# Experts' down product in plain float32 with four column groups, and the steps around it, in a two-block network on one core

## Chip, cores and metric

One core of a Trainium2 chip runs the whole program. The metric is the device time of one execution in microseconds. A profiled execution gives a trace besides; its times are from its first to its last instruction.

## The reference

Two blocks of two layers each work on 256 tokens of 1024 features in float32. Only the last layer's last step matters here, a mixture of eight experts with 1536 hidden features of which each token takes two:

```python
def swiglu(h, w_gate, w_up, w_down):
    return (jax.nn.silu(h @ w_gate) * (h @ w_up)) @ w_down

def moe_swiglu(h, router, w_gate, w_up, w_down):
    probs = jax.nn.softmax((ht @ router).astype(F32), axis=-1)
    top_p, top_i = lax.top_k(probs, TOP_K)
    top_p = top_p / jnp.sum(top_p, axis=-1, keepdims=True)
    gates = jnp.sum(jax.nn.one_hot(top_i, N_EXPERTS, dtype=F32) * top_p[..., None], axis=1).astype(h.dtype)
    for e in range(N_EXPERTS):
        out = out + gates[:, e:e + 1] * swiglu(ht, w_gate[e], w_up[e], w_down[e])
```

## The kernel before

All products but one kind are computed in three float32r matmuls (`mm3`, lines 312 to 316): both operands are split into a high part (a copy by ACT) and a low part (a subtraction by DVE), and high x high, high x low and low x high are summed in PSUM. `wload` (lines 298 to 310) loads a weight unit into a `raw` buffer (three of 8 KB per partition) and splits it into `wh` and `wl` buffers (five each of 4 KB). The exception is the experts' up product, which is in plain float32 already.

The experts' layer is `moe` (from line 1379). For each expert at most CAP = 96 tokens are gathered with a one-hot matrix `oh`; if an expert has more, the program runs `experts` again with a base of 96 and of 192, each behind a branch (`tc.If`, line 1652). With these inputs neither branch is taken. The loop at line 1614 orders the work of expert `e`:

- `up(e)`, line 1518: the gathered tokens `xg` (features on partitions, 96 tokens as three tiles of 32) are the stationary operand, and the weights stream. Four column groups of 32 of the array work on four column ranges of 384 weights at once. Sixteen `mw` tiles (8 k steps of gate and up weights, 768 KB each, 512 KB for expert 0) are loaded by SP into seven buffers. Its six PSUM banks ("up" banks) are then all full; SiLU on ACT and a product on DVE empty them into three `u` tiles.
- Beside `up(e)` stand `scatter(e - 2)` (line 1596), which brings an expert's rows back to the tokens with two matmuls each for the high and low part, and updates `x` with the gate on DVE, and for every odd `e` the gather of the next pair of experts (line 1500), both in a second set of two banks ("dn"). They are called at odd k steps.
- `down(e - 1)`, line 1570: 12 blocks of 128 hidden features; per block two halves of 512 output columns, each an `mm3` with the turned hidden features (`ph`, `pl`, 128 x 96) as the stationary operand, so 72 matmuls. At its end `oh` is turned (`ohT`), and the two accumulators are split into `yh` and `yl`.
- `turn(e)`, line 1542: nine transposes bring the `u` tiles to features on partitions, through three "up" banks, and a split makes `ph` and `pl`. The following `up(e + 1)` uses the same banks.

After the loop come `down(7)`, in it `scatter(6)`, and then `scatter(7)`, which also writes the output. The order of PE's instructions is that of the code (`manual_schedule` with `MAN`); the order on ACT, DVE and on SP, which issues the loads, is a planner's. Every engine takes its own instructions in order. `places` makes the one-hot tiles, and `first_up` computes the first third of expert 0's hidden features for all tokens before the loop.

Of the kernel before, what the change touches and what calls it, by code (L numbers as in the profile page):

```python
# [37 lines left out]
MW_BUFS = 7  # L38
# [140 lines left out]
def pack(i):  # L179
# [32 lines left out]
    a["mo_d"] = units_cols(i["moe_down_2"][0].reshape(NE * DE, D), 2, D)  # L212
# [10 lines left out]
def build(tc, a, out, stages=None):  # L223
# [7 lines left out]
    with ExitStack() as es:  # L231
# [1147 lines left out]
        def moe(more, head, next_head):  # L1379
            hT = nrm["h"]  # L1380
            with tc.tile_pool(name="moe", bufs=1) as sp:
# [74 lines left out]
                def first_up(mid):  # L1456
# [15 lines left out]
                    for t in range(2):  # L1472
                        u = sp.tile([P, 512], F32, tag="u", name="u", bufs=4)
# [13 lines left out]
                def experts(base, mid):  # L1487
# [10 lines left out]
                    xg, made, turned, back = {}, {}, {}, {}  # L1498

                    def gather(e, kind="dn"):  # L1500

                        xg[e // 2] = xgs[e // 2 % 2]
                        for k0 in range(0, KT, 2):
                            p = bank(kind)
# [8 lines left out]
                            for k in (k0, k0 + 1):  # L1513
                                src = grp(p[:, (k - k0) * S : (k - k0 + 1) * S], 2)[:, :, :CAP]
                                A.activation(xg[e // 2][:, k], src, AF.Copy, scale=nrm["g"][:, k : k + 1])
                            yield

                    def up(e):
# [4 lines left out]
                        h = xg[e // 2]  # L1523
                        o = [[bank("up") for _ in range(2)] for _ in range(NT)]
                        for k in range(KT):
                            for m in range(2):
                                w = sp.tile([P, DE], F32, tag="mw", name="mw", bufs=MW_BUFS)
                                nc.sync.dma_start(w[:, : 4 * n], a["mo_u"][(e * KT + k) * 2 + m][:, lo:])
                                for t in range(NT):
                                    l = h[:, k, e % 2, t * C32 : (t + 1) * C32]  # L1530
                                    for g in range(4):
                                        T.matmul(o[t][m][g * C32 : (g + 1) * C32, :n], l, w[:, g * n : (g + 1) * n],  # L1532
                                                 start=k == 0, stop=k == KT - 1, skip_group_check=True)
                            yield
                        made[e] = []
                        for t in range(NT):
                            u = sp.tile([P, 384], F32, tag="u", name="u", bufs=4)
# [4 lines left out]
                    def turn(e):  # L1542

                        ph = sp.tile([P, DE // P, CAP], F32R, tag="ph", name="ph", bufs=2)
                        pl = sp.tile([P, DE // P, CAP], F32R, tag="pl", name="pl", bufs=2)
                        turned[e] = (ph, pl)
                        k1 = 0
                        if e in mid:
                            k1 = 4
                            u = mid[e]  # L1550
                            for k0 in (0, 2):
# [9 lines left out]
                                split(ph[:, k0 : k0 + 2], pl[:, k0 : k0 + 2], grp(p, 2)[:, :, :CAP])  # L1561
                        c = (DE // P - k1) // 4
                        for t, u in enumerate(made.pop(e)):
# [3 lines left out]
                            part = lambda z: z[:, k1:, t * C32 : (t + 1) * C32].rearrange("p (g c) n -> p c g n", c=c)  # L1567
# [122 lines left out]
```

## Time and profile before

| | us |
|---|---|
| median of three runs (1708.68 to 1712.89) | 1708.85 |
| the profiled execution's own time | 1710.19 |
| its span, first to last instruction | 1708.3 |
| PE busy | 1636.6 (96%) |
| DVE busy | 1014.3 (59%) |
| ACT busy | 830.2 (49%) |
| DMA bytes | 335.11 MB, 196 GB/s over the span |

The rows below are of these views. The page's slices cut the span into 40 parts; a digit is the busy share in tenths. A row of the windows gives a stretch in us, its length, then for PE, PEld (weight loads), DVE, ACT and POOL the busy time with the number of instructions in brackets (engines without any are left out where a row is of one line alone), then PE's granted clock as a share of full speed, the busy share of the 16 DMA engines, and GB/s. A row of a timeline gives start, duration, engine, line and operation, what it writes from what, shapes and count, and in square brackets how long the engine stood idle before it and who ended that. A row of the chain gives start, duration and the step that the end hung on. A row of the waits gives who waited for whom, the total in us, how often, and the longest. Matmuls overlap in the records: the distance of their starts is what one costs, not the duration that is shown. A float32 product leaves two matmul records.

### The profile page before, as it was taken

What the parts mean: (1) busy time and instruction counts of PE and PEld (TensorE: products, weight loads), DVE (VectorE), ACT (ScalarE), POOL (GpSimd) and SP (SyncE); (2) the same over time, 40 slices, a digit from 0 to 9 for tenths busy, and PEclk for the clock granted to TensorE, in tenths of its full rate; (3) what the DMA queues carried; (4) which work ended last, traced back from release to release, by engine and by line L of the source; (5) the groups of instructions that cost most, each with busy time, mean ns of one, the idle gap of its engine ahead of it and who ended that gap; (6) DMA issues with size and microseconds to landing.
All of it is one profiled execution on the core that took longest, in us unless ns stands there. A gap on an engine that the chain in (4) does not pass through costs nothing.

```text
span 1708.3 us, 28919 instructions
## 1 busy us (share of the span) xinstructions
PE 1636.6 (96%) x11932; PEld 1323.4 (77%) x11932; DVE 1014.3 (59%) x1653; ACT 830.2 (49%) x1428; POOL 135.8 (8%) x158
## 2 busy tenths in 40 slices
PE   7999999999999999989999999989899999999995
PEld 5878999888889998989899998979764455445554
DVE  6767777676487776876565555875641344234434
ACT  6646555555475565653464445653532234124323
POOL 2100000021000001260000001440100000000000
PEclk9999999999999999989999999999999999999998
DMA  7433655455245544530265544410479998989963
GB/s 278 148 122 134 214 177 194 148 206 173 99 151 198 190 175 151 171 110 1 77 231 187 189 169 156 168 67 24 181 276 366 334 347 336 355 315 327 359 234 111
DMA packets 52580, 335.11 MB, mean 196 GB/s; under 512 B 6000, under 2 KB 6032, under 8 KB 25680
## 3 DMA queue, kind: packets, MB, share of 16 engines
q1 hardware_dynamic: 51120, 327.70, 53.2%
q0 software_dynamic: 736, 4.32, 0.7%
q8 instruction: 97, 1.59, 0.4%
q10 hardware_dynamic: 576, 1.08, 0.2%
q14 instruction: 51, 0.42, 0.1%
HBM read 332.03 MB, written 1.05 MB: 195 GB/s over the span
## 4 chain that ended last, share of the span: by engine, by line
PE 81%; DVE 5%; issue 5%; ACT 3%; DMA 3%; POOL 2%; DVEq 0%; ACTq 0%; POOLq 0%
PE pj L316 13%; PE pj L315 13%; PE pj L314 13%; PE pj L1532 9%; PE sm L314 5%; PE sm L316 5%; PE sm L315 5%; PE sm L1532 5%; DVE wl L307 2%; DMA raw<-in_mo_d 2%; PE sm L425 2%; PE sm L1151 2%; PE sm L1160 2%; ACT wh L306 1%; PE sm L1154 1%
## 5 line engine op out<-in xcount | busy, mean ns | idle before, releaser
L307 DVE TENSOR_TENSOR wl<-raw,wh 128x1024 fp32r<-128x1024 f32 (+2 forms) x448 | 538.1, 1212 | 228.5 <-ACT wh L306 224.4
L306 ACT CAST wh<-raw 128x1024 fp32r<-128x1024 f32 (+2 forms) x448 | 458.9, 1033 | 277.2 <-PE pj L315 102.2
L314 PE MATMUL pj<-hTh,wh 128*128 128x256 f32 x1192 | 336.1, 282 | 0.0
L315 PE MATMUL pj<-hTl,wh 128*128 128x256 f32 x1192 | 335.8, 282 | 0.0
L316 PE MATMUL pj<-hTh,wl 128*128 128x256 f32 x1192 | 335.3, 282 | 0.0
L314 PEld LDWEIGHTS pj<-hTh,wh 128*128 128x128 f32 x1192 | 227.1, 191 | 1.1
L315 PEld LDWEIGHTS pj<-hTl,wh 128*128 128x128 f32 x1192 | 227.2, 191 | 0.9
L316 PEld LDWEIGHTS pj<-hTh,wl 128*128 128x128 f32 x1192 | 226.8, 191 | 0.2
L1532 PE MATMUL pj<-mw,xg 128*32 128x384 f32 (+1 forms) x2048 | 183.7, 475 | 8.1 <-DVE pl L321 4.8
L314 PE MATMUL sm<-wh,ph 128*128 128x512 f32 (+1 forms) x456 | 179.7, 394 | 3.2 <-ACT ph L320 3.2
L315 PE MATMUL sm<-wl,ph 128*128 128x512 f32 (+1 forms) x456 | 179.3, 393 | 0.0
L316 PE MATMUL sm<-wh,pl 128*128 128x512 f32 (+1 forms) x456 | 177.8, 393 | 1.2 <-DVE pl L321 1.2
L1532 PEld LDWEIGHTS pj<-mw,xg 128*32 128x32 f32 x2048 | 64.3, 110 | 100.9 <-issue 81.3
L316 PE MATMUL pj<-wh,hTl 128*128 128x512 f32 (+1 forms) x368 | 137.9, 377 | 3.3 <-DVE hTl L328 3.3
L314 PE MATMUL pj<-wh,hTh 128*128 128x512 f32 (+1 forms) x368 | 139.2, 381 | 0.5 <-ACT hTh L326 0.4
L315 PE MATMUL pj<-wl,hTh 128*128 128x512 f32 (+1 forms) x368 | 137.5, 376 | 0.2 <-DVE wl L307 0.2
L1532 PE MATMUL sm<-mw,xg 128*32 128x384 f32 (+1 forms) x1024 | 102.3, 478 | 3.0 <-DVE pl L321 3.0
L314 PEld LDWEIGHTS sm<-wh,ph 128*128 128x128 f32 (+1 forms) x456 | 80.8, 177 | 30.4 <-issue 3.4
L316 PEld LDWEIGHTS sm<-wh,pl 128*128 128x128 f32 (+1 forms) x456 | 80.8, 177 | 25.5 <-DVE pl L321 1.6
L315 PEld LDWEIGHTS sm<-wl,ph 128*128 128x128 f32 (+1 forms) x456 | 80.7, 177 | 22.6
L836 DVE SCALAR_TENSOR_TENSOR u<-pj,tab_f,u 128x254 f32<-128x254 f32 (+1 forms) x176 | 82.8, 479 | 20.0 <-ACT u L834 18.2
L316 PEld LDWEIGHTS pj<-wh,hTl 128*128 128x128 f32 x368 | 69.5, 189 | 15.6 <-DVE hTl L328 6.1
(418 smaller groups left out, 2198.7 us busy)
## 6 DMA issues: line engine op xcount, KB each, us to landing
mw<-in_mo_u SPq DMA_DIRECT2D x112, 768.0 KB, 6.7
raw<-in_mo_d SPq DMA_DIRECT2D x48, 1024.0 KB, 5.3
raw<-in_up SPq DMA_DIRECT2D x44, 1024.0 KB, 4.8
raw<-in_dn SPq DMA_DIRECT2D x22, 1024.0 KB, 4.8
raw<-in_fg_u SPq DMA_DIRECT2D x22, 1024.0 KB, 4.8
raw<-in_od_b SPq DMA_DIRECT2D x18, 1024.0 KB, 4.8
raw<-in_hy_b SPq DMA_DIRECT2D x16, 768.0 KB, 4.3
raw<-in_hy_a SPq DMA_DIRECT2D x12, 1024.0 KB, 4.9
```

What stands on the lines that cost most here:

```text
L306: A.copy(h, r)
L307: V.tensor_sub(m, r, h.bitcast(F32))
L314: T.matmul(o, lh, rh, start=first, stop=False)
L315: T.matmul(o, lh, rl, start=False, stop=False)
L316: T.matmul(o, ll, rh, start=False, stop=last)
L425: T.matmul(q, hT[j][:, k, ts_], w[f][k][v], start=t + k + i == 0, stop=k == KT - 1 and i == 2, skip_group_check=True)
L836: V.scalar_tensor_tensor(u[:, g, sh:], q[:, : S - sh], cw[:, f, g, wi : wi + 1], u[:, g, sh:], op0=OP.mult, op1=OP.add)
L1151: T.matmul(pq[:, i * P : (i + 1) * P], Am[:, i], U[:, i], start=i == 0, stop=True, skip_group_check=True)
L1154: T.transpose(pt[:, i * P : (i + 1) * P], U[:, i], ident)
L1160: T.matmul(pu[:, i * P : (i + 1) * P], Tt[:, i], Q[:, i], start=i == 0, stop=True, skip_group_check=True)
L1532: T.matmul(o[t][m][g * C32 : (g + 1) * C32, :n], l, w[:, g * n : (g + 1) * n], start=k == 0, stop=k == KT - 1, skip_group_check=True)
```

## The change

`mo_d` is packed as plain rows of 128 x 1024 per block. The down product is float32 in four column groups: for each of the 12 blocks, four products of 512 columns (two tiles of 32 tokens x two halves of the output) into one bank, and four of 256 columns (the third tile of 32 tokens) into the other. Down weights are not split any more; they are loaded as 1 MB pairs into `raw` and as single 512 KB blocks into the `wh` and `wl` buffers. `turn` makes one float32 tile `uT` with ACT copies, and also turns the one-hot. The gather of the next pair and `turn(e)` are called inside `down(e - 1)`, in the "up" banks; half of the gather's evictions are on DVE. The accumulators are gathered into one tile `y` before the split into `yh` and `yl`. There are 8 `mw` buffers instead of 7, 3 `u` buffers instead of 4, and one `xg` tile instead of two. In the last expert the order of the last blocks is no longer a special one. The second overflow branch stands inside the first.

```diff
-MW_BUFS = 7
+MW_BUFS = 8
+Q = D // 4
...
-    a["mo_d"] = units_cols(i["moe_down_2"][0].reshape(NE * DE, D), 2, D)
+    a["mo_d"] = np.ascontiguousarray(i["moe_down_2"][0]).reshape(-1, P, D)
...
-                    def gather(e, kind="dn"):
-
-                        xg[e // 2] = xgs[e // 2 % 2]
+                    def gather(e):
+
                         for k0 in range(0, KT, 2):
-                            p = bank(kind)
+                            p = bank("up")
...
-                                A.activation(xg[e // 2][:, k], src, AF.Copy, scale=nrm["g"][:, k : k + 1])
+                                A.activation(o, src, AF.Copy, scale=g) if k0 % 4 else V.tensor_scalar_mul(o, src, g)
...
+                    def product(o, l, w, first, last):
+                        T.matmul(o, l, w, start=first, stop=last, skip_group_check=True)
...
-                                split(ph[:, k0 : k0 + 2], pl[:, k0 : k0 + 2], grp(p, 2)[:, :, :CAP])
+                                A.copy(uT[:, k0 : k0 + 2], grp(p, 2)[:, :, :CAP])
...
-                            split(part(ph), part(pl), p[:, : c * P].rearrange("p (c g n) -> p c g n", c=c, g=4))
...
+                            A.copy(uT[:, k1:, t * C32 : (t + 1) * C32].rearrange("p (g c) n -> p c g n", c=c),
+                                   p[:, : c * P].rearrange("p (c g n) -> p c g n", c=c, g=4))
...
-                            if w[kk] is None:
-                                w[kk : kk + 2] = wload(a["mo_d"][e * nk // 2 + kk // 2], 2, D)
-                            c = slice(n * 512, (n + 1) * 512)
-                            mm3(acc[n][:CAP], ph[:, kk], pl[:, kk], w[kk][0][:, c], w[kk][1][:, c], kk == 0, kk == nk - 1)
...
+                        for kk in range(nk):
+                            if kk % 4 == 0:
+                                raw = wbuf("raw", 2 * D, F32, RAW_BUFS)
+                                nc.sync.dma_start(grp(raw, 2), a["mo_d"][e * nk + kk : e * nk + kk + 2].rearrange("k p c -> p k c"))
+                                w += [raw[:, :D], raw[:, D:]]
+                            elif kk % 4 >= 2:
+                                one = wbuf(("wh", "wl")[kk % 2], D, F32, W_BUFS)
+                                nc.sync.dma_start(one, a["mo_d"][e * nk + kk])
+                                w.append(one)
+                            for g in range(4):
+                                t, c = g % 2, g // 2 * H
+                                product(acc[0][g * C32 : (g + 1) * C32], uT[:, kk, t * C32 : (t + 1) * C32],
+                                        w[kk][:, c : c + H], kk == 0, kk == nk - 1)
+                            for g in range(4):
+                                product(acc[1][g * C32 : (g + 1) * C32, :Q], uT[:, kk, 2 * C32 :], w[kk][:, g * Q : (g + 1) * Q],
+                                        kk == 0, kk == nk - 1)
+                            if kk % 2:
+                                yield
...
+                        y = sp.tile([P, D], F32, tag="y", name="y", bufs=1)
+                        A.copy(y[: 2 * C32, :H], acc[0][: 2 * C32])
+                        V.tensor_copy(y[: 2 * C32, H:], acc[0][2 * C32 :])
+                        for g in range(4):
+                            o, p = y[2 * C32 : CAP, g * Q : (g + 1) * Q], acc[1][g * C32 : (g + 1) * C32, :Q]
+                            V.tensor_copy(o, p) if g % 2 else A.copy(o, p)
+                        split(yh[:CAP], yl[:CAP], y[:CAP])
...
                         for k, _ in enumerate(up(e)):
                             if k % 2 == 1:
                                 next(side, 0)
                                 next(side, 0)
-                        rest(side)
+                        more_ = gather(e + 1) if e % 2 == 1 and e + 1 < NE else iter(())
                         if e:
-                            rest(down(e - 1))
-                        turn(e)
+                            for k, _ in enumerate(down(e - 1)):
+                                next(more_, 0)
+                                if k == 3:
+                                    turn(e)
+                        else:
+                            turn(e)
...
-                for base in (CAP, 2 * CAP):
-                    with tc.If(full > base):
+                with tc.If(full > CAP):
+                    with tc.manual_schedule(engines=MAN):
+                        experts(CAP, {})
+                    with tc.If(full > 2 * CAP):
                         with tc.manual_schedule(engines=MAN):
-                            experts(base, {})
+                            experts(2 * CAP, {})
```

## Rows read from the trace of the kernel before

**Rows 1.** The page's 40 slices: PE and DMA, busy tenths.

```profile
PE   7999999999999999989999999989899999999995
...
DMA  7433655455245544530265544410479998989963
```

**Rows 2.** Windows over the experts' loop: ups 0 and 1; the six middle experts.

```profile
1258.00:1316.40 58.40, 58.40 (x815) 30.54 (x807) 4.01 (x10) 8.36 (x21) 0.00 (x0) 1.00 0.97 369
1316.40:1649.80 333.40, 322.30 (x2918) 164.28 (x2914) 128.37 (x145) 102.32 (x142) 0.00 (x0) 0.99 0.89 331
```

**Rows 3.** Windows of 8 us: first 512 KB loads, then 768 KB loads.

```profile
1268.00:1276.00 8.00, 8.00 (x154) 4.81 (x148) 0.00 (x0) 0.00 (x0) 0.00 (x0) 1.00 1.01 387
1276.00:1284.00 8.00, 8.00 (x102) 4.95 (x98) 2.98 (x8) 2.62 (x8) 0.00 (x0) 1.00 1.01 417
```

**Rows 4.** Windows of line 1532 alone: an unhindered quarter, then six first quarters.

```profile
1346.53:1354.41 7.88, 7.88 (x96) 3.01 (x96) 1.00 0.96 364
1334.34:1345.40 11.06, 8.29 (x96) 2.81 (x96) 1.00 0.98 351
1389.13:1399.68 10.55, 8.29 (x96) 2.81 (x96) 1.00 0.95 344
1447.91:1456.85 8.94, 8.08 (x96) 2.93 (x96) 1.00 0.95 335
1500.58:1513.33 12.75, 9.96 (x96) 3.06 (x96) 0.87 0.86 295
1561.54:1570.55 9.01, 8.09 (x96) 2.91 (x96) 1.00 0.96 333
1614.29:1624.09 9.80, 8.29 (x96) 2.81 (x96) 1.00 0.98 367
```

**Rows 5.** PE's timeline at the start of up(3).

```profile
1390.75 0.85 PE L1532 MATMUL pj<-mw,xg 128*32 128x384 f32 x8 [0.76 <-ACT ohT L1589]
1393.09 2.14 PE L1532 MATMUL pj<-mw,xg 128*32 128x384 f32 x24 [1.49 <-DVE pl L321]
```

**Rows 6.** The chain that ended last, just ahead of these.

```profile
1387.47 1.06 ACT wh L306
...
1388.55 2.36 DVE wl L307 x2
```

**Rows 7.** The DMA queue's own waits, 1200 to 1708 us.

```profile
SPq L301 <- DVE wl L307: 177.2, 50, 17.1
```

**Rows 8.** A down product's window, line 314 alone (one of three).

```profile
1371.15:1387.84 16.69, 9.49 (x24) 3.86 (x24) 1.00 0.91 343
```

**Rows 9.** Windows of line 1532: 256 columns (up 0), 384 columns (half of up 2).

```profile
1257.23:1278.08 20.85, 20.85 (x384) 12.37 (x384) 1.00 0.98 373
1355.54:1371.15 15.61, 15.61 (x192) 6.13 (x192) 1.00 0.96 361
```

**Rows 10.** PE's timeline at the start of down(7).

```profile
1671.06 0.47 PE L314 MATMUL sm<-wh,ph 128*96 128x512 f32 x1 [3.17 <-ACT ph L320]
...
1672.93 0.74 PE L316 MATMUL sm<-wh,pl 128*96 128x512 f32 x1 [1.17 <-DVE pl L321]
1673.46 0.63 PE L314 MATMUL sm<-wh,ph 128*96 128x512 f32 x1
```

**Rows 11.** Window of one scatter insertion, line 1603 alone (half of it).

```profile
1399.68:1400.81 1.13, 0.89 (x2) 0.37 (x2) 1.00 0.60 178
```

**Rows 12.** Timelines of DVE and PE before up(0).

```profile
1251.93 3.51 DVE L307 TENSOR_TENSOR wl<-raw,wh 128x1024 fp32r<-128x1024 f32 x3
...
1256.09 0.38 PE L1509 MATMUL pj<-oh,xh 128*128 128x256 f32 x1 [1.30 <-DVE u L1475]
```

**Rows 13.** Timelines of ACT and DVE at the end.

```profile
1692.51 0.58 ACT L320 CAST yh<-sm 96x512 fp32r<-96x512 f32 x1 [2.19 <-PE sm L316]
...
1694.19 2.73 DVE L1605 SCALAR_TENSOR_TENSOR x<-pj,gates,x 128x512 f32<-128x512 f32 x4 [0.38 <-PE pj L1604]
```

**Rows 14.** SP's own waits at the branches.

```profile
SPq L1652 <- SPq L1652: 6.9, 2, 3.9
```

More of the change, by code (lines that the diff above doesn't have):

```diff
@@ L1542, in turn @@
                     def turn(e):
[L1544 to L1546 removed]
+                        uT = sp.tile([P, DE // P, CAP], F32, tag="uT", name="uT", bufs=2)
+                        turned[e] = uT
                         k1 = 0
@@ L1589, in down @@
                         A.copy(ohT[:CAP], p[:CAP, :S].rearrange("p (t n) -> p t n", t=2))
-                        yh = sp.tile([P, 2, 512], F32R, tag="yh", name="yh", bufs=1)
-                        yl = sp.tile([P, 2, 512], F32R, tag="yl", name="yl", bufs=1)
-                        for n in range(2):
-                            split(yh[:CAP, n], yl[:CAP, n], acc[n][:CAP])
-                        back[e] = (ohT, yh, yl)
+                        back[e] = ohT
+                    def down(e):
+                        uT = turned.pop(e)
+                        acc = [bank("dn"), bank("dn")]
+                        nk = DE // P
+                        H = 2 * Q
+                        w = []
+                        for kk in range(nk):
[16 more added lines that the diff above has]
+                                yield
+                        yh = sp.tile([P, D], F32R, tag="yh", name="yh", bufs=1)
+                        yl = sp.tile([P, D], F32R, tag="yl", name="yl", bufs=1)
+                        y = sp.tile([P, D], F32, tag="y", name="y", bufs=1)
[5 more added lines that the diff above has]
+                        split(yh[:CAP], yl[:CAP], y[:CAP])
+                        back[e] = (back[e], yh, yl)
@@ L1609, in scatter @@
                                 yield
-                    rest(gather(0, "up"))
+                    rest(gather(0))
                     for e in range(2, NE):
@@ L1614, in experts @@
                     for e in range(NE):
-                        side = iter(())
-                        if e >= 2:
-                            side = scatter(e - 2)
-                        if e % 2 == 1 and e + 1 < NE:
-                            side = chain(side, gather(e + 1))
+                        side = scatter(e - 2) if e >= 2 else iter(())
                         for k, _ in enumerate(up(e)):
@@ L1646, in moe @@
                 banks["dn"] = ([ps() for _ in range(2)], 0)
-                xgs = [xp.tile([P, KT, 2, CAP], F32, tag=tag, name="xg", bufs=2) for tag in ("xTh", "xTl")]
+                xg = xp.tile([P, KT, 2, CAP], F32, tag="xTh", name="xg", bufs=2)
                 with tc.manual_schedule(engines=MAN):
```

33 lines of the change are left out of this document (10 added, 23 removed).

## The prediction

> **What bounds the kernel now.** I read the page's slices first. PE is busy nearly everywhere, and only in the last quarter do DMA's digits also stand at 8 and 9 [rows 1]. That quarter is the experts' loop (1257 to 1692 us), the only part that the change touches, so the question is which of PE and DMA ends last there. The windows by stretch answer it: over the six middle experts (1316.4 to 1649.8) PE is busy 322.3 of 333.4 us, while DMA moves 331 GB/s at a share of 0.89 [rows 2]. The same DMA moved 417 GB/s between 1276 and 1284, where free buffers let the queue run full [rows 3]. So PE is the bound and DMA has room. Per expert the queue moves 16 x 0.786 + 12 x 0.524 = 18.9 MB: 45 us at 417 GB/s, where an expert takes 333.4 / 6 = 55.6 us.
>
> Why, then, is PE idle some 11 us there? The windows of the up product show it. A quarter of an up product (96 records; every plain float32 product leaves two) takes 7.88 us when nothing holds it, but the first quarter of ups 2 to 7 takes 8.94 to 12.75 [rows 4]. PE's timeline names the holder: the records wait for ACT's ohT copy (0.76 us) and DVE's pl split (1.49 us) [rows 5], that is, for the PSUM banks that `turn` has just filled. The chain of work says why these come late: in front of pl stand the copies and subtractions (wh 1.06, wl 2 x 1.18 us) of the down weights for the next expert, which ACT and DVE take in order [rows 6]. SP's loads wait for the same wl splits, 177.2 us in all [rows 7], which costs nothing while PE is the bound.
>
> **The change part by part.** (1) Down product. Now 72 matmuls in 16.69 us, 0.232 us each, of which one of three lines has 24 [rows 8]. After: per block kk four products of 512 columns and four of 256, each two records. The price of a record in four column groups: 20.85 / 384 = 54.3 ns for 256 columns, 15.61 / 192 = 81.3 ns for 384 [rows 9]. The step of 27.0 ns per 128 columns puts 512 at 108.3 ns. A block is 8 x 108.3 + 8 x 54.3 = 1301 ns, an expert 12 x 1.301 = 15.61 us: 1.08 us less, for eight experts **-8.6**. No row has 512 columns in four groups; the bounds are 81.3 ns (as at 384) and 0.232 us (today's 512-column record). I take 108.3, since the two rows lie on a line through almost zero.
>
> (2) The splits of the down weights go: per expert 12 on ACT and 12 on DVE. Neither engine is the bound, so their time itself brings nothing; what they delay does. The turn becomes plain ACT copies and stands after the eighth of twelve blocks of `down(e-1)`, so its evictions have four blocks (5.2 us) of product behind them before an up product needs the banks. The first quarters of rows 4 sum to 62.11 us against 6 x 7.88 = 47.28: **-14.8**. The cover is those four blocks; without it the bank waits are back. Bounds: -14.8 and, if half comes back at other banks, -7.4.
>
> (3) Start of `down(7)`. Its weights were turned immediately before: idle 3.17 and 1.17 us, then half a dozen records about 0.2 us slower than the rest, lasting 0.63 us where 0.47 and less stood before the pause (1.2 us) [rows 10]: **-5.7**. In its place a new wait: `down(7)` follows `down(6)` with nothing between, and both accumulators must be copied out first (0.6 us for the 512 columns, like yh in rows 13); after two blocks `scatter(6)` needs yl, some 3.5 us after `down(6)`'s last record while 2.6 us of product cover it. Queued behind on PE is everything up to the end, so both count: **+1.2** (0 to 3).
>
> (4) Gather goes from inside the up product (two insertions per pair) into the down product (four, the last shared with the turn). The matmuls are the same. An insertion costs its switches: a scatter pair of four matmuls takes 1.13 us [rows 11] against 4 x 0.232 = 0.93, so 0.2 us; one more for each of three gathers: **+0.6**. Gather, turn and one-hot issue no DMA, so no queue is crossed. Their evictions, half of gather's now on DVE, are hidden by the product blocks. That `xg` is one tile costs nothing: gather writes it after `up(e)`, its last reader, has ended.
>
> (5) Ahead of the loop DVE no longer has three wl splits (3.51 us) in front of the u product for which gather(0) waits 1.30 us [rows 12]: **-1.3** (0 to -2.5, since other splits between 1215 and 1257 go too).
>
> (6) The very end. Now 4.41 us from ACT's first yh split to the end of the last update (1692.51 to 1696.92) [rows 13]. After: the accumulators go through `y` in six pieces (the four 32x256 ones an estimated 0.3 to 0.4 each, between nothing and yh's 0.58, two per engine), then yh and yl over all 1024 columns (1.06 and 1.18 us [rows 6]) one after the other, then scatter and four updates (2.73 us [rows 13]): 1.0 + 1.06 + 1.2 + 0.5 + 2.73 = 6.5, and up to 7.4 if PE's records are slow after the pause, as in rows 10. I take **+2.5** (1.5 to 5). In the other experts `up(e+1)` covers this: the scatter begins two of its steps, 3.9 us, in, and the copies end after about 3.3.
>
> (7) The nested branch: SP waits twice at the branch line, 6.9 us in all, the longest 3.9 [rows 14]. One of two jumps goes: **-3.4** (-3.9 to 0, if something else ends the program).
>
> (8) Loads. Same bytes, but 9 per expert instead of 6, half of the down bytes in 512 KB pieces, and 8 `mw` buffers. No wait for a split is left, so SP issues as soon as PE frees a buffer. With 8 tiles (6.3 MB) and at least 12 blocks ahead, the queue may lag 15 us before PE feels it. The 512 KB loads of up(0) ran at 387 GB/s, the 768 KB ones after them at 417 [rows 3]: 1.36 and 1.89 us a load, so about 0.3 us of fixed time each and 24 x 0.3 = 7 us over the whole loop, spread over a queue with about 7 us to spare per expert: **0**.
> The Trainium skill (DMA: Bandwidth & Descriptors, Bandwidth) speaks against this part: it advises loads of at least 1 MiB and counts smaller ones as losing to a fixed cost, about 2.0 us per transfer in its fit. Taken as queue time this would be 24 x 2.0 = 48 us, an estimate from that page, and the second rival below would come true. By the rows just named the fixed part overlaps with other loads.
>
> **Sum:** -8.6 - 14.8 - 5.7 + 1.2 + 0.6 - 1.3 + 2.5 - 3.4 = -29.5 us. The sum is made on the profiled span (1708.3 us; that execution's own time was 1710.19, the median of the runs 1708.85). From the median: **1679 us**.
>
> **Rivals.** *Waits move.* The six `up` banks that `up(e)` has just filled now serve gather and turn within the same down product; if silu, product and eviction don't empty them in time, PE waits again inside the block sequence. Half of (2) is lost: 1679 + 7.4 = 1687. For it: ACT and DVE keep their order from a planner, as now. Against: each bank has at least two blocks (2.6 us) before its next use, against about 0.5 us per eviction.
> *DMA takes over.* From 1258 on, 4.2 + 88.1 MB of `mw` and 44 MB of down weights are still to come (8 tiles and 12 blocks being there). At 369 GB/s, the rate of 1258 to 1316 [rows 2], the last lands at 1627, well ahead of PE. At only 331 it lands at 1670; two blocks, the end of (6) and 8 us of program end follow: 1691. For it: today's 331 may be the queue's own pace. Against: today's loads wait for splits [rows 7], and the queue has shown 417.
> *Slower.* The 512-column float32 products in the first accumulator don't overlap as those of 384 do. There are 8 x 12 x 8 = 768 such records; the change turns slower than before once each costs 29.5 / 768 = 38 ns more, 147 instead of 108 ns. If they cost double, as two groups at a time would, it is 768 x 0.108 = 83 us: 1762. Against: 256 and 384 lie on one line; for it: nothing but that the width is unseen.
> *The branch does nothing*: without (7), 1683; inside the forecast's own range.
>
> **How the numbers follow.** Chances: forecast (1672 to 1685) 0.67, waits move 0.15, DMA 0.09, slower 0.06, faster than 1670 for reasons I don't see 0.03. The range for 8 in 10 takes in the first three for the most part: 1670 to 1693. A change of 0.3% (5 us) is about what a measurement of this kernel can tell from none: faster by more 0.91, within 0.03, slower 0.06.
>
> **What would show it.** Right: up's first quarters at 7.9 us; a down product with its turn at 16.9 us and with gather at 21.3; no ACT or DVE releaser at the start of an up; 512-column records 108 ns apart; one branch wait of SP. Wrong: PE waiting for DMA inside an up or down (second rival), for ACT or DVE inside a down (first), records at 147 ns or more (third). The forecast falls if PE waits for loads at all, since then no PE time saved counts.

## The result, and the profile after

The changed kernel takes 1681.51 us (median of four runs, 1680.43 to 1682.36), the one before, run beside it on the same chip, 1708.76 us: a ratio of 0.9834 with a 95% interval of 0.9817 to 0.9851. In the profiled executions, on which the sum was made, the times are 1710.19 and 1680.69 us and the spans 1708.3 and 1678.8 us: 29.5 us less in both, the predicted sum. The medians differ by 27.2 us, since the profiled run before lay 1.4 us above its median and the one after 0.8 below; against the forecast of 1679 us, made from the median, the median came out 2.5 us longer.

First the slices of the page of the changed kernel, PE and DMA in busy tenths.

```profile
PE   7999999999999999999999999989999999999997
...
DMA  7433555555326554440155554540279999999962
```

Where DMA's digits in the loop's quarter had 8s among them [rows 1], they now stand at 9, and PE's stand at 9 in both but for the last slice. Which of the two ends last is read from the windows: first of the kernel before from the first record of up(0) to just before the last of up(7), then of the changed kernel over its loop and over ups 0 and 1 (columns: window, its length, busy time and instructions of PE, PEld, DVE, ACT and POOL, granted clock, DMA share, GB/s).

```profile
1257.23:1649.40 392.17, 381.07 (x3733) 195.33 (x3736) 132.52 (x154) 111.35 (x164) 0.00 (x0) 1.00 0.91 337
```

```profile
1255.44:1627.10 371.66, 371.66 (x4455) 164.17 (x4458) 49.74 (x82) 42.31 (x93) 0.00 (x0) 1.00 0.94 356
...
1258.00:1316.40 58.40, 58.40 (x820) 28.93 (x812) 3.67 (x8) 4.35 (x12) 0.00 (x0) 1.00 1.02 413
```

The stretch that took PE 392.2 us with 11.1 us idle now takes 371.7 us with none. DVE's busy time there falls from 132.5 to 49.7 us, ACT's from 111.4 to 42.3. The queue moves 413 GB/s over ups 0 and 1, where [rows 2] had 369.

The starts of the first and last records of the two traces cut the gain into stretches (negative is less time):

| stretch | before | after | difference | predicted |
|---|---|---|---|---|
| span's start to up(0) | 1257.23 | 1255.44 | -1.8 | -1.3 |
| up(0) to the last record of up(7) | 392.20 | 371.68 | -20.5 | -6.5 - 14.8 + 0.6 = -20.7 |
| from there to the last product record of down(7) | 42.66 | 36.68 | -6.0 | -2.2 - 5.7 + 1.2 = -6.7 |
| from there to the end of the last update | 4.83 | 9.16 | +4.3 | +2.5 |
| from there to the end of the span | 11.41 | 5.86 | -5.5 | -3.4 |
| sum | | | -29.5 | -29.5 |

(Six down products lie in the second stretch and two in the third, 1.08 us each. The stretches go by the starts of records and the ends of updates.)

The windows of the product line alone, in the changed kernel: four blocks of a down product with the first quarter of up(3) behind them, and a later quarter of the same up product.

```profile
1377.30:1390.34 13.04, 13.04 (x160) 5.10 (x160) 1.00 1.00 377
1391.46:1399.34 7.88, 7.88 (x96) 3.02 (x96) 1.00 0.96 351
```

13.04 less 4 blocks of 1.29 us leaves 7.88 for a first quarter, as the free one beside it; in [rows 4] first quarters took 8.94 to 12.75. PE's timeline of the same stretch (start, duration, operation, count) shows the records running from down into up without a releaser, where [rows 5] had waits for ohT and pl.

```profile
1365.52 2.76 PE L1520 MATMUL sm<-raw,uT 128*32 128x512 f32 x32
1368.10 1.47 PE L1520 MATMUL sm<-wh,uT 128*32 128x512 f32 x16
...
1375.95 1.20 PE L1567 MATMUL pj<-tab_com,u 128*128 128x128 f32 x9
...
1377.30 2.79 PE L1520 MATMUL sm<-raw,uT 128*32 128x512 f32 x32
...
1382.48 0.83 PE L1520 MATMUL sm<-mw,xg 128*32 128x384 f32 x8
```

(A group's form is that of its first record; a block of a down product is 8 records of 512 and 8 of 256 columns.) Two blocks take 2.58 us by their starts (1365.52 to 1368.10), so twelve take 15.48, where the prediction had 15.61 and [rows 8] 16.69. From its first record to that of the next up product (1365.52 to 1382.48) this down product with its turn takes 16.96 us, as forecast (16.9). SP's own waits after the change, 1200 to 1680 us, now name PE, which frees buffers; the splits that held loads for 177.2 us in [rows 7] are gone (what is left on DVE's wl, like the 16.4 us here, are splits of the stage before, the last of which begins at 1237.1, ahead of the loop).

```profile
SPq L1531 <- PE pj L1520: 112.0, 72, 4.5
SPq L1588 <- PE sm L1520: 82.1, 21, 18.9
...
SPq L1588 <- DVE wl L308: 16.4, 3, 10.5
...
SPq L1669 <- SPq L1669: 4.1, 2, 3.0
```

The last of these is the branch: still two waits, 4.1 us in all, where [rows 14] had 6.9.

The two places where PE waits in the changed kernel lie at the start of down(7) and at the very end. First PE's timeline at the start of down(7) (in brackets the idle time before and what ended it), which answers to [rows 10]:

```profile
1643.10 1.47 PE L1520 MATMUL sm<-wl,uT 128*32 128x512 f32 x16
1645.63 1.06 PE L1520 MATMUL sm<-raw,uT 128*32 128x512 f32 x8 [1.05 <-DVE y L1607]
1646.93 1.93 PE L1520 MATMUL sm<-raw,uT 128*32 128x256 f32 x24 [0.24 <-DVE y L1610]
```

The last block of down(6) is done at 1643.10 + 1.29 = 1644.39, so down(7) begins 1.24 us late. Then the timeline of the end, all engines, which answers to [rows 13]:

```profile
1663.82 0.58 ACT L1606 COPY y<-sm 64x512 f32<-64x512 f32 x1 [15.86 <-PE sm L1520]
1664.42 0.36 ACT L1610 COPY y<-sm 32x256 f32<-32x256 f32 x1
1664.43 0.69 DVE L1607 COPY y<-sm 64x512 f32<-64x512 f32 x1 [11.90 <-ACT y L1606]
1665.15 0.42 DVE L1610 COPY y<-sm 32x256 f32<-32x256 f32 x1
1665.61 0.36 ACT L1610 COPY y<-sm 32x256 f32<-32x256 f32 x1 [0.82 <-DVE y L1610]
1666.00 0.43 DVE L1610 COPY y<-sm 32x256 f32<-32x256 f32 x1 [0.43 <-ACT y L1610]
1666.47 1.04 ACT L321 CAST yh<-y 96x1024 fp32r<-96x1024 f32 x1 [0.50 <-DVE y L1610]
1667.54 1.22 DVE L322 TENSOR_TENSOR yl<-y,yh 96x1024 fp32r<-96x1024 f32 x1 [1.11 <-ACT yh L321]
...
1667.56 0.79 PE L1621 MATMUL pj<-yh,ohT 96*128 96x512 f32 x1 [3.38 <-ACT yh L321]
...
1669.65 3.31 DVE L1623 SCALAR_TENSOR_TENSOR x<-pj,gates,x 128x512 f32<-128x512 f32 x4 [0.89 <-PE pj L1622]
```

### The profile page after: what moved, and what is told of

It reads as the page before. It is cut to its first block, busy times and chain, and to the rows that moved or that the text cites. A ratio compares the mean times of both kernels' runs of the same rounds, so it can differ in the third digit from the quotient of the medians.

```text
span 1678.8 us, 30586 instructions
## 1 busy us (share of the span) xinstructions
PE 1625.6 (97%) x12892; PEld 1280.6 (76%) x12892; DVE 906.5 (54%) x1563; ACT 737.2 (44%) x1332; POOL 135.8 (8%) x158
## 3 DMA queue, kind: packets, MB, share of 16 engines
q10 hardware_dynamic: 576, 1.08, 0.2%
## 4 chain that ended last, share of the span: by engine, by line
PE 87%; issue 4%; DVE 3%; ACT 2%; POOL 2%; DMA 1%; POOLq 0%; ACTq 0%; DVEq 0%
PE pj L317 13%; PE pj L315 13%; PE pj L316 13%; PE sm L1520 12%; PE pj L1520 9%; PE sm L317 4%; PE sm L315 4%; PE sm L316 4%; PE sm L426 2%; PE sm L1152 2%; PE sm L1161 2%; DVE wl L308 1%; PE sm L1155 1%; ACT wh L307 1%; POOL qa L1238 1%
## 5 line engine op out<-in xcount | busy, mean ns | idle before, releaser
L308 DVE TENSOR_TENSOR wl<-raw,wh 128x1024 fp32r<-128x1024 f32 (+1 forms) x352 | 422.6, 1208 | 182.2 <-ACT wh L307 180.5
L307 ACT CAST wh<-raw 128x1024 fp32r<-128x1024 f32 (+1 forms) x352 | 359.7, 1028 | 216.5 <-PE pj L316 100.6
L316 PE MATMUL sm<-wl,ph 128*128 128x512 f32 x264 | 103.2, 391 | 0.0
L315 PE MATMUL sm<-wh,ph 128*128 128x512 f32 x264 | 103.1, 391 | 0.0
L317 PE MATMUL sm<-wh,pl 128*128 128x512 f32 x264 | 102.0, 391 | 0.0
L315 PEld LDWEIGHTS pj<-wh,hTh 128*128 128x128 f32 x368 | 69.8, 190 | 11.9 <-ACT hTh L327 2.5
L316 PEld LDWEIGHTS pj<-wl,hTh 128*128 128x128 f32 x368 | 69.7, 190 | 9.2
L835 ACT ACTIVATE u<-pj,tab_f 128x256 f32<-128x256 f32 x88 | 49.1, 561 | 48.9 <-DVE u L837 48.9
```

What stands on the lines that cost most here:

```text
L307: A.copy(h, r)
L308: V.tensor_sub(m, r, h.bitcast(F32))
L315: T.matmul(o, lh, rh, start=first, stop=False)
L316: T.matmul(o, lh, rl, start=False, stop=False)
L317: T.matmul(o, ll, rh, start=False, stop=last)
L835: A.activation(u[:, g], q, AF.Identity, bias=cw[:, f, g, 3:4], scale=cw[:, f, g, 2:3])
```

## The experiments

The gain splits by stretch nearly as predicted. Left open by the two traces are the reasons: what removed the waits at the first quarters (the four blocks behind the turn, or the missing splits), what the end costs and why, what the branch is worth, and how much room the queue has. The three kernels on the queue and the two with fewer tiles ran once each; the other times are medians, with the range of the runs in brackets, and ratios are to runs of the kernel before beside them.

### The branch alone

The branches side by side again, all else as changed.

```diff
-                with tc.If(full > CAP):
-                    with tc.manual_schedule(engines=MAN):
-                        experts(CAP, {})
-                    with tc.If(full > 2 * CAP):
+                for base in (CAP, 2 * CAP):
+                    with tc.If(full > base):
                         with tc.manual_schedule(engines=MAN):
-                            experts(2 * CAP, {})
+                            experts(base, {})
```

> The changed kernel with the second overflow branch after the first again instead of inside it; nothing else differs. Theory (each branch that is not taken costs a jump on the engine that ends last, 3.0 to 3.9 us): 3 to 4 us slower than the changed kernel, about 1685 us, with two waits of SP at the branch line of some 7 us together. Rival (something else ends the program, the landing of the output for instance): no difference, 1681 to 1682 us.

Measured: 1685.25 us (1683.38 to 1685.73), a ratio to before of 0.9865 (95% interval 0.9842 to 0.9887, and so for the ratios below), against 1681.51 with the nested branch. From the last update to the end of the span it is 9.08 us, with the nested branch 5.86: the second jump costs 3.2 us. SP's own wait at the branch line in this kernel:

```profile
SPq L1670 <- SPq L1670: 6.6, 2, 3.6
```

6.6 us, near the 6.9 of [rows 14], against 4.1 in the changed kernel. What this run doesn't explain is the rest: before, the same stretch took 11.41 us, so 2.3 us of the 5.5 have another cause.

### The turn after the down product

The product as changed, without splits, but the turn where it was, behind `down(e - 1)`.

```diff
                             for k, _ in enumerate(down(e - 1)):
                                 next(more_, 0)
-                                if k == 3:
-                                    turn(e)
-                        else:
-                            turn(e)
+                        turn(e)
```

> The changed kernel with the turn (and its one-hot part) back between the down product and the next up product; the product itself, the unsplit weights and the gather's place stay. Theory 1 (the wait goes because four blocks of product cover the evictions): PE waits again at the start of ups 2 to 7 and of the last down product, 1 to 2 us each, 7 to 14 us in all, 1689 to 1695 us. Theory 2 (the splits of the down weights ahead of the evictions on ACT and DVE were the holder, and they are gone): at most 3 us slower, 1682 to 1684.5 us.

Measured: 1679.80 us (1679.24 to 1681.70), ratio 0.9835 (0.9813 to 0.9858; the change has 0.9834): no slower than the change, and a little faster than either theory had it. PE's timeline at the start of an up product in this kernel, and the window of that first quarter on the product line:

```profile
1330.11 0.88 PE L1567 MATMUL pj<-tab_com,u 128*128 128x128 f32 x6
...
1331.15 0.38 PE L1572 MATMUL sm<-tab_com,oh 128*96 128x128 f32 x2
1331.46 1.50 PE L1520 MATMUL pj<-mw,xg 128*32 128x384 f32 x16
```

```profile
1331.46:1339.34 7.88, 7.88 (x96) 3.02 (x96) 1.00 0.96 335
```

The up product follows its turn at once, with no cover, and its first quarter takes 7.88 us. The other ups are as free: all that PE itself waits for, from 1260 to 1660 us, is one line, at the start of `down(7)`.

```profile
PE sm L1520 <- DVE y L1610: 0.2, 1, 0.2
```

So with the splits gone the four blocks behind the turn are not what removes the wait. Two things went with the splits, and this run doesn't tell them apart: the copies and subtractions of the weights that stood in front of the turn's evictions [rows 6], and the second half of each of these evictions itself (`ph` and `pl` were a copy and a subtraction, `uT` is one copy). The stretch from up(0) to the last record of up(7) is 372.52 us, 0.84 longer than in the change; the next one is 35.66 us, 1.02 shorter, since the turn between `down(6)` and `down(7)` covers the copies that `down(7)` waits for.

### The move alone, in the kernel before

The other half: splits and product as before, only the turn moved inside the down product, four of twelve blocks ahead of its end.

```diff
-                            if (kk, n) == (3, 1):
+                            if (kk, n) in ((3, 1), (7, 1)):
                                 yield
...
                         if e:
-                            rest(down(e - 1))
-                        turn(e)
+                            for k, _ in enumerate(down(e - 1)):
+                                if k == 1:
+                                    turn(e)
+                        else:
+                            turn(e)
```

> The kernel before with one edit: the turn is called after the eighth of the twelve blocks of the old, split down product; splits, gather, banks, branches as before. Theory 1 (cover): the bank waits of 14.8 us at the starts of the ups and most of the 5.7 us at the start of the last down product go, since four blocks at 1.39 us cover the evictions: 1690 to 1697 us. Theory 2 (the splits hold the evictions wherever the turn stands): within 4 us of the kernel before, 1705 to 1710 us.

Measured: 1691.72 us (1689.58 to 1694.63), ratio 0.9906 (0.9880 to 0.9932), against 1707.96 of the kernel before beside it: 16.2 us less. From up(0) to the last record of up(7) it is 377.45 us instead of 392.20: 14.75 us, the whole term (2), with the splits still there. The span's start to up(0) is 0.75 us shorter, and the stretches from the last product record on are as before (within 0.2 us); the stretch with `down(7)` is 38.42 instead of 42.66 us. PE's waits from 1260 to 1660 us, first all of the kernel before, then all of this one, the latter in `down(7)`:

```profile
PE pj L1532 <- DVE pl L321: 4.8, 4, 1.5
PE pj L1532 <- ACT ohT L1589: 3.3, 3, 1.3
PE sm L1532 <- DVE pl L321: 3.0, 2, 1.5
```

```profile
PE sm L314 <- DVE yl L321: 1.6, 1, 1.6
```

So either edit alone removes the bank waits, and the second then adds nothing to that term. The prediction had one of the two as the reason and the other as what makes it possible.

### The end in halves

In the end's timeline above, copies out of different accumulators overlap (ACT's second, from 1664.42, and DVE's first, from 1664.43), while copies out of the same one go in turn: DVE's first begins 0.03 us after ACT's first has ended, and of the four of 256 columns the last two each begin when the other engine's is done (1665.57 to 1665.61, 1665.97 to 1666.00). Here each accumulator has one engine, and the split goes by halves of 512 columns.

```diff
-                        A.copy(y[: 2 * C32, :H], acc[0][: 2 * C32])
-                        V.tensor_copy(y[: 2 * C32, H:], acc[0][2 * C32 :])
-                        for g in range(4):
-                            o, p = y[2 * C32 : CAP, g * Q : (g + 1) * Q], acc[1][g * C32 : (g + 1) * C32, :Q]
-                            V.tensor_copy(o, p) if g % 2 else A.copy(o, p)
-                        split(yh[:CAP], yl[:CAP], y[:CAP])
+                        for n in range(2):
+                            c = slice(n * H, (n + 1) * H)
+                            A.copy(y[: 2 * C32, c], acc[0][n * 2 * C32 : (n + 1) * 2 * C32])
+                            for g in (2 * n, 2 * n + 1):
+                                V.tensor_copy(y[2 * C32 : CAP, g * Q : (g + 1) * Q], acc[1][g * C32 : (g + 1) * C32, :Q])
+                            split(yh[:CAP, c], yl[:CAP, c], y[:CAP, c])
```

> The changed kernel with another way out of the accumulators: ACT copies both parts of the first bank, DVE the four parts of the second, and the split into yh and yl goes by halves of 512 columns. In the changed kernel the six copies run one after the other, ACT and DVE waiting for each other in turn: 2.65 us from the first copy's start to the start of yh, where 1.0 was predicted, and 9.1 us from there to the last update's end. Theory (this chain is the missing part of the end term, and the same chain holds the start of the last down product for some 1.3 us): 2 to 4 us faster, 1677.5 to 1679.5 us. Rival (DVE's four updates and the pace of PE after its pause set the end): less than 1 us.

Measured: 1679.11 us (1677.50 to 1681.28), ratio 0.9832 (0.9807 to 0.9856). The timeline of this kernel's end:

```profile
1662.62 1.19 ACT L1608 COPY y<-sm 64x512 f32<-64x512 f32 x2 [15.98 <-PE sm L1520]
1663.05 1.74 DVE L1610 COPY y<-sm 32x256 f32<-32x256 f32 x4 [11.71 <-PE sm L1520]
1663.99 0.62 ACT L321 CAST yh<-y 96x512 fp32r<-96x512 f32 x1 [0.18 <-DVE y L1610]
...
1664.66 0.50 PE L1621 MATMUL pj<-yh,ohT 96*128 96x512 f32 x1 [1.68 <-ACT yh L321]
...
1666.25 2.86 DVE L1623 SCALAR_TENSOR_TENSOR x<-pj,gates,x 128x512 f32<-128x512 f32 x4
```

The copies now overlap, and PE stands idle 1.68 us before the scatter instead of 3.38. From the last product record to the end of the last update it is 6.51 us instead of 9.16, and 0.7 us come off ahead of it (35.94 against 36.68), where `down(7)` waits for the same copies. The two profiled spans differ by 3.3 us, the medians by 2.4; the ranges of the runs touch, so the stretches carry this reading more than the medians do.

Part of the difference goes with PE's clock. The windows of the scatter at the end, first of the changed kernel, then of this one in two parts, then of the kernel before:

```profile
1667.50:1672.00 4.50, 3.97 (x8) 2.46 (x8) 3.36 (x4) 0.01 (x1) 0.00 (x0) 0.50 0.16 58
```

```profile
1664.60:1666.60 2.00, 1.54 (x5) 1.04 (x6) 1.92 (x4) 0.62 (x2) 0.00 (x0) 0.92 0.00 0
1666.60:1668.50 1.90, 1.73 (x5) 0.81 (x3) 1.85 (x4) 0.00 (x0) 0.00 (x0) 0.50 0.36 123
```

```profile
1692.50:1696.90 4.40, 2.31 (x10) 1.43 (x8) 3.40 (x5) 0.85 (x2) 0.00 (x0) 1.00 0.25 91
```

The granted clock is 1.00 (2.4 GHz) before the change, where PE had stood 0.72 us; 0.50 (1.2 GHz) for the whole scatter after it, behind 3.38 us idle; and with halves, behind 1.68 us, it falls when four of the scatter's eight records are done. At 1.00 these records begin 0.23 us apart, at 0.50 0.43 us. An update of `x` needs two of them: before the change the updates begin 0.66 us apart, more than the 0.46 of two records, and after it 0.85 us apart, which is what two records now take. The four updates take 2.73 us [rows 13], 3.31 and 2.86 us. The edit gives each bank to one engine and also halves the split; what each is worth alone was not run.

### Both together

The turn after the down product and the end in halves (the two edits above, no others).

> Both edits that were as fast as the changed kernel or faster: the turn between the products again, and the accumulators emptied bank by bank and in halves. Theory (their effects are at different places, about 1 us at the turn and the head and 3 us at the end, and add up): 1676 to 1679 us, span 1673 to 1676. Rival (with the turn after the down product its copies queue behind the emptying of the accumulators on ACT, and now more so): 1680 to 1684 us, with PE waiting for ACT at the starts of the ups.

Measured: 1678.42 us (median of five, 1678.09 to 1681.17), ratio 0.9822 (0.9799 to 0.9846). It has the lowest median of all, but it can't be told from the halves alone. Its waits of PE's weight loads at the starts of the up products are small:

```profile
PEld sm L1520 <- ACT uT L1568: 3.3, 7, 0.7
PEld pj L1520 <- ACT uT L1568: 3.0, 9, 0.6
```

At most 0.7 us each, beside PE's running records. The stretch from up(0) to the last record of up(7) is 373.21 us, 1.5 longer than in the change; that is what giving up the cover behind the turn costs in this kernel, and the stretches behind it, 41.69 against 45.84 us up to the end of the last update, give more than that back.

### The queue alone

The rival in which DMA takes over hung on whether 331 GB/s was the queue's own pace. Here PE has too little to do to hold it: of the up products, the tokens' second and third tile are multiplied in the first step only.

```diff
-                                for t in range(NT):
+                                for t in range(1 if k else NT):
                                     for g in range(4):
                                         product(o[t][m][g * C32 : (g + 1) * C32, :n], xg[:, k, e % 2, t * C32 : (t + 1) * C32],
-                                                w[:, g * n : (g + 1) * n], k == 0, k == KT - 1)
+                                                w[:, g * n : (g + 1) * n], k == 0, k == (KT - 1 if t == 0 else 0))
```

> The changed kernel with most of the up product left out: the second and third tile of 32 tokens are multiplied at the first of eight k steps alone, so PE needs some 34 us per expert while every load stays. Theory (the queue has room: 18.9 MB per expert at 413 to 417 GB/s are 45 to 46 us against PE's 53): the loop becomes as fast as the loads, 136 MB from 1257 us on in about 330 us, and the program takes 1600 to 1615 us. Rival (the 341 GB/s of the changed kernel's six middle experts is the queue's own pace): 400 us of loads, 1670 to 1682 us.

Measured: 1637.25 us, between the two expectations. The window from 1257.6 to 1580 us and PE's waits from 1260 to 1660:

```profile
1257.60:1580.00 322.40, 264.88 (x2651) 102.43 (x2650) 48.47 (x81) 39.37 (x90) 0.00 (x0) 0.92 1.01 410
```

```profile
PE sm L1520 <- DMA mw<-in_mo_u: 41.0, 43, 4.2
PE pj L1520 <- DMA mw<-in_mo_u: 17.3, 18, 1.8
```

Now PE does wait for loads, and the queue moves 410 GB/s throughout. The last `mw` tile lands at 1582 us, so in the changed kernel, whose loop ends at 1627, the queue has about 45 us of room over the whole loop. The rival of an own pace near 341 GB/s, the rate of the changed kernel's queue from 1315 to 1640 us, falls:

```profile
1315.00:1640.00 325.00, 325.00 (x3769) 139.88 (x3765) 47.18 (x76) 37.45 (x82) 0.00 (x0) 1.00 0.91 341
```

That the time came out above what the theory gave is a step I left out: behind the last up tile PE still has `down(6)`, `down(7)` and the end to do, some 55 us.

### More loads into the queue

Does a load have a fixed price in queue time, as term (8) estimated with 0.3 us? On top of the kernel just shown, each `mw` load is cut in two. First by partitions:

```diff
-                                nc.sync.dma_start(w[:, : 4 * n], a["mo_u"][(e * KT + k) * 2 + m][:, lo:])
+                                for s in (slice(0, 64), slice(64, P)):
+                                    nc.sync.dma_start(w[s, : 4 * n], a["mo_u"][(e * KT + k) * 2 + m][s, lo:])
```

> As the run before (most of the up product left out), with each load of up weights in two, 64 partitions each, the same bytes and row lengths: 128 more loads. The difference of the two is the queue time of a load by itself. By the prediction's rows, 0.3 us of fixed time each: 35 to 40 us longer than the run before. If the fixed part overlaps wholly: within 5 us of it. By the fit that the Trainium skill (DMA: Bandwidth & Descriptors, Bandwidth) gives, about 2.0 us each, an estimate from that page: some 250 us longer.

Measured: 1817.38 us, 180 us more than with whole loads. The same window:

```profile
1257.60:1580.00 322.40, 200.00 (x1792) 73.88 (x1780) 32.76 (x55) 25.76 (x61) 0.00 (x0) 0.72 1.02 272
```

The DMA engines are busy throughout at 272 GB/s: the same 6 KB packets take some 400 ns each (median) instead of 236. This says what loads of 64 partitions cost, not what a load costs, and left the question open. So each load was cut by columns instead, with all 128 partitions and rows of 3 KB:

```diff
-                                nc.sync.dma_start(w[:, : 4 * n], a["mo_u"][(e * KT + k) * 2 + m][:, lo:])
+                                for s in range(0, 4 * n, 2 * n):
+                                    nc.sync.dma_start(w[:, s : s + 2 * n], a["mo_u"][(e * KT + k) * 2 + m][:, lo + s : lo + s + 2 * n])
```

> As e4_queue_alone (most of the up product left out), with each load of up weights in two by columns: all 128 partitions, rows of 3 KB instead of 6 KB, 128 more loads. In the run with halves by partitions a packet of 6 KB took 406 ns instead of 240, so that run measured what 64 partitions cost and not the fixed time of a load. From the packets of e4_queue_alone (161 ns for 4 KB, 236 for 6 KB in the median) 3 KB would take some 124 ns, 4% slower per byte. Theory (a load has no queue time of its own, only its rows do): 5 to 15 us longer than the 1637 us of e4_queue_alone. By the prediction's 0.3 us per load on top: 43 to 53 us longer. By the 2.0 us per transfer of the Trainium skill's fit (DMA: Bandwidth & Descriptors, Bandwidth), an estimate from that page: some 260 us longer.

Measured: 1644.15 us, 6.9 us more than with whole loads, and in the same window:

```profile
1257.60:1580.00 322.40, 292.85 (x2622) 113.67 (x2615) 48.48 (x81) 39.29 (x90) 0.00 (x0) 0.97 1.03 401
```

128 loads more for 6.9 us are 0.05 us per load. That is one run against one, on different chips, and the kernel before varied by 8 us from run to run (1706.22 to 1714.55), so the price is small rather than known: 0.1 us per load would be 13 us. The traces themselves agree with the times: the last up tile lands at 1589.5 instead of 1582. The median packet of 3 KB took 124 ns, that of 6 KB 236: 41 and 39 ns per KB, 5% more. On the up weights still to come, some 88 MB or 215 us at 410 GB/s, 5% would be 11 us. So the shorter rows can account for all that was measured, and a fixed price per load doesn't show.

### Four tiles, and seven

The change also adds an eighth `mw` buffer. One edit, `MW_BUFS = 4` and `MW_BUFS = 7` in place of 8.

> The changed kernel with 4 tiles for the up weights instead of 8. Theory (PE never waits for a load because 8 tiles are 15 us of up product ahead, and a load lands some 7 us after its issue): 4 tiles, 7.8 us ahead, are just at the edge, and PE waits for loads now and then: 1683 to 1700 us. Rival (the number of tiles is of no account at this pace): 1680 to 1683 us.

> The changed kernel with 7 tiles for the up weights, as in the kernel before, instead of 8. Theory (7 tiles are 13.6 us of up product ahead, a load lands some 7 us after its issue): no difference, 1680 to 1683 us, and no wait of PE for a load in the ups. Rival (the eighth tile carries part of the gain, as the 22 us lost with 4 tiles suggest by 5 us per tile): 1685 us or more.

Measured: 1703.54 us with four, 1681.96 with seven. With four, the list of PE's waits from 1260 to 1660 us has loads in it:

```profile
PE sm L1520 <- DMA mw<-in_mo_u: 12.5, 18, 1.9
PE pj L1520 <- DMA mw<-in_mo_u: 3.9, 6, 1.5
```

With seven there is no wait of PE for DMA, and up(0) to the last record of up(7) takes 371.68 us, as with eight. Four tiles are too few, slightly more so than was expected: the stretch is 23.1 us longer, of which this list names 16.4. The eighth carries nothing that shows.

## Why the prediction came out right, and where its steps did not

(1) *Down product.* Right. 54.3 and 81.3 ns for 256 and 384 columns [rows 9] lie on a line that holds at 512: a block takes 1.29 us by its starts, predicted 1.301, and a record of 512 columns 107 ns, predicted 108.3. This rules out the slower rival, which needed 147 ns.

(2) *First quarters, -14.8.* The size is right: 7.88 us, no releaser of ACT or DVE, and each of ups 2 to 7 takes 33.5 us from its first record to that of the next product. The reason given ("the cover is those four blocks; without it the bank waits are back") is half of it. Without the cover, but without splits too, the waits stayed away (turn after the down product, 1679.80 us); with the splits but with the cover they went as well (the move alone, 14.75 us less). The chain of [rows 5] and [rows 6] had two links, the turn late on PE and splits ahead of and within its evictions, and cutting either is enough. The rival of moved waits therefore had more against it than the prediction gave it.

(3) *Start of down(7).* The old pauses went, as said; the parts named for them add up to 3.17 + 1.17 + 1.2 = 5.5, not 5.7. The new wait measured more than its +1.2: `down(7)` starts 1.24 us late, and its second accumulator some 0.4 us (1645.63 + 8 x 0.107 = 1646.49 to 1646.93): 1.7 us, within the 0 to 3. It hangs on the same chain of copies as (6), and halves take 0.7 us of it.

(4) *Insertions.* Undersized. In the move alone, where no bank wait disturbs it, a gather in the up product cost 4.2 to 4.4 us (37.86 and 38.03 from the first record to that of the next product, against 33.62 without one); in the changed kernel's down product it costs 4.8 (21.78 against 16.97; 21.3 was forecast). For three gathers that is some 1.5 us instead of 0.6. In the second stretch it hardly shows, because its six down products at 15.48 instead of 15.61 us give 0.8 back: the stretch misses its sum by 0.2.

(5) *Ahead of the loop.* -1.8 instead of -1.3, within its bounds.

(6) *The end.* This term was mis-sized: +4.3 instead of +2.5. By its own working, 6.5 us from the first copy to the last update became 9.14. The copies were priced at 1.0 us, two engines side by side; they took 2.65 (1663.82 to 1666.47), in turn. The scatter and updates were priced at 0.5 + 2.73 and took 0.89 + 3.31, at a granted clock of 0.50; the prediction had named this case ("up to 7.4") without taking it. One reading was wrong: the 4.41 us of before begin with ACT's second `yh` split, not its first. The first half of the accumulators was split beside the last products (the last product record starts at 1692.09), which the old order of the last blocks allowed:

```profile
1690.35 0.69 DVE L321 TENSOR_TENSOR yl<-sm,yh 96x512 fp32r<-96x512 f32 x1 [2.46 <-ACT yh L320]
```

This leaves the sum as it is, but the change gave that overlap up, and no run tried the new product with the old order. The Trainium skill (PSUM — Partial Sum Buffer, PSUM bank collisions raise a hardware error) has two engines at one bank as something that programs must order, though only where both touch the same 32 partitions of it. The copies here read different partitions of one bank and still went in turn, each released by the other engine's copy; whether they could have run at once no run tried, since the halves went round it by giving each bank one engine.

(7) *The branch.* The second jump is 3.2 us, predicted 3.4. The stretch gained 5.5, and the remaining 2.3 are not settled: with the branches side by side in the changed kernel the end is still 2.3 us shorter than before, while SP's own waits there are nearly the same (6.6 and 6.9 us). Of the 2.3 us, 1.7 lie between SP's first two instructions at the program's last line: 1.8 us before (1704.93 to 1706.72), 0.06 with the branches side by side in the changed kernel, but 1.6 in the move alone, which has the old branches and the old product. What holds SP there is not shown. That the profile would show one wait instead of two was wrong: two are there, shorter.

(8) *Loads.* Nothing, as said, but not for the reason given. The estimate of 0.3 us of fixed time per load compared the 512 KB loads of up(0) with later 768 KB ones [rows 3], and these differ in row length too: rows of 4 KB and of 6 KB. In the queue alone such packets take 162 and 236 ns (medians), and a load is eight for each of the 16 DMA engines: 1.30 and 1.89 us, which leaves 3 x 1.30 - 2 x 1.89 = 0.1 us of the 0.3. Most of the 0.3 was thus the one window of 8 us at 387 GB/s. The column halves found about 0.05 us for one load more, rows included. By the Trainium skill's fit weighed in the prediction (DMA: Bandwidth & Descriptors, Anatomy of one DMA — SWDGE (gpsimd) path: about 2.0 us fixed per transfer, measured on DMAs that GpSimd issues, where here SP does), 128 loads more would have cost 256 us of queue time, an estimate from that page; the run shows 6.9. The rival that DMA takes over also fell: the queue alone held 410 GB/s. (The 1691 us given for it add up to some 1689 by its own figures: 1670 + 2.6 + 6.5 + 8, and 1.9 from the span to the time.)

So the mechanism held in its main terms, but that the sum came out to a tenth is luck, because errors cancelled: the end cost 1.8 us more than its term, the stretch with `down(7)` 0.7 and the loop 0.2, while the branch's stretch gave 2.1 more and the head 0.5. It is also the luck of the two profiled executions; by the medians 27.2 of the 29.5 us came.

## What to carry to other kernels

A wait that ends with a late eviction can be cut at either end, by moving the producer earlier under other work or by emptying the queue of the evicting engine; test each alone before paying for both. When accumulators are drained at the end, where nothing covers it, giving each PSUM bank to one engine and going in halves paid here, and copies that share a bank are priced one after the other unless a trace shows otherwise. A rate that a queue shows while its consumer frees the buffers says nothing of its own pace: take the consumer's work away once and read it.

## What the runs showed of the hardware

In one run, loads of 64 partitions each, in pairs, moved 272 GB/s with the DMA engines at a share of 1.02, where whole loads of 128 partitions moved 410 at a share of 1.01; the packets of up weights were of the same 6 KB and took some 400 instead of 236 ns. And plain float32 records in four column groups cost 54, 81 and 107 ns for 256, 384 and 512 columns, in proportion to the columns.
